# Two heads stored by GpSimd in four row pieces, and mask codes of the upper nodes in eight rows: a tree attention kernel on one Trainium2 core

## The chip, the core and the metric

The kernel runs on one core of a Trainium2 chip. The core has a tensor engine for matrix products (PE in the profile; PEld is its weight load, which overlaps the products), a vector engine (DVE), a scalar engine (ACT), GpSimd (POOL) and a sync engine (SP) that here only issues transfers. The engines work on SBUF, a memory of 128 partitions; products land in PSUM. Inputs and output lie in the chip's main memory, and 16 DMA engines move data between it and SBUF. A DMA is issued by SP, ACT or POOL, which each have a queue of their own, and signals through a semaphore when its data has landed. The metric is the device time of one execution in microseconds (us); less is better.

## What is computed

The reference is attention with a tree mask: 8 batches of 12 heads, 512 positions, dimension 64, all fp32. Positions are the nodes of a binary tree in heap order, and each position sees itself and its ancestors only.

```python
    for i in range(seq):
        mask[i, i] = 1
        parent = i
        while parent > 0:
            parent = (parent - 1) // 2
            mask[i, parent] = 1

    scores = np.einsum('bhqd,bhkd->bhqk', Q, K) * scale
    scores = scores + (1 - mask) * (-1e9)
    weights = np.exp(scores - np.max(scores, axis=-1, keepdims=True))
    weights = weights / (np.sum(weights, axis=-1, keepdims=True) + 1e-10)
    return np.einsum('bhqk,bhkd->bhqd', weights, V).astype(np.float32)
```

## The kernel before

The 96 heads are worked off as 48 pairs. `Q`, `K` and `V` are loaded by GpSimd with a cast to bf16, heads in groups of 2 to 16, into buffers of the pools `loads` and `vloads` (L238 to L302). For each pair the tensor engine transposes the rows of `K` and `Q` (L398 to L549), computes scores in two parts, turns them into outputs with the values (`values`, L650), and the vector engine divides by the sums (`norm`, L692) into the output tiles `ofs`, one per eight heads, fp32.

The mask is made by products, not by an addition. For every node a column of plus and minus 2048 stands for its path from the root, and a row product with the query's path is 0 where the key is an ancestor and far below 0 elsewhere. This product with the codes opens each accumulation in PSUM, and the product of keys and queries is added to it. Keys are split in two parts: the upper nodes (`scores1`: path codes of at most 7 bits and one row more, `k1code` or `k1wide` with `q1code`) and the nodes below (`scores2`: four tiles with ten rows of codes each, 40 in all, `k2code` or `k2wide` with `q2code`). `_mask_codes` (L71) makes one table of 1536 columns; its first `CODE_ROWS` = 40 rows are loaded into the tile `codes` by two DMAs of SP, 32 and 8 rows (L190). ACT then copies the 40 rows to partitions 64 to 103, since the two heads of a pair use partitions 0 and 64 upwards: 1280 columns at the start (L214), the last 256 at the step "W" (L881). For the later pairs, `far_codes` (L390) makes a copy of the query codes in another column order; both halves of the partitions and both parts make four copies on ACT (L822). The upper part's products take all 40 rows (L567 to L572), of which rows 8 to 39 of `k1` and `q1` are zero.

The order of the work is written out by hand: `FIRST` and the string in the main loop (L861 to L867) give the steps of each pair, and `pool_program` (L725) is one list of all that GpSimd does: loads, copies of values (`spread_pool`, `spread_top`), copies of staged rows (`lay_beside`) and stores. `pool(i)` (L843) takes items off the head of this list as long as `ready` (L773) allows it, so GpSimd's order is fixed. A store of GpSimd takes eight heads of all 128 partitions, 1 MB: in the output each partition holds 1 KB of a head. A store waits until `norm` has written its heads.

Heads 72 to 79 are handled apart. Their pairs are (72, 76), (73, 77), (74, 78) and (75, 79). `store_apart` (L719), called after pair step 38, lets SP store heads 72 and 73 early, each in two DMAs of partitions 0 to 115 and 116 to 127. GpSimd stores the other six heads, 74 to 79, in one DMA (L762 to L765: `n` is 2 there). Its last store is that of heads 80 to 87. Heads 88 to 95 are stored by SP (L897 to L903) and, the very last, by ACT (L904), pair by pair.

Of the kernel before, what the change touches and what calls it, by code (L numbers as in the profile page):

```python
# [9 lines left out]

CODE = 2048.0
CODE_ROWS = 40
NOUT = 22
BEHIND = 56

# [55 lines left out]
def _mask_codes():  # L71
# [5 lines left out]
    k1 = np.zeros((64, 128), np.float32)  # L77
    q1 = np.zeros((64, 4, 128), np.float32)
# [20 lines left out]
    for t in range(4):  # L99
# [4 lines left out]
        for p in range(128):  # L104
            node = 4 * p + t
            query(q1, 0, 7, (PLACE[t], p), node)
            if p >= 32:
                query(q2, 10 * (SELF[t] if p < 64 else t), 9, (PLACE[t], p), node)
    return np.concatenate([k1, q1.reshape(64, -1), k2, q2.reshape(64, -1), k1w, k2w], axis=1)


EYE = ((0, 1, 2), (2, 3, 2), (6, -2, -1), (0, 3, 2), (1, 2, 1))
# [7 lines left out]
def kernel(  # L120
# [7 lines left out]
    nc = tc.nc  # L128
# [26 lines left out]

    perm_dram = nc.inline_tensor(_eye_twice().astype(ml_dtypes.bfloat16), name="tree_eye")
    code_dram = nc.inline_tensor(
        _mask_codes()[0:CODE_ROWS].astype(ml_dtypes.bfloat16), name="tree_codes"
    )

    ctx.enter_context(tc.manual_schedule())
# [25 lines left out]
    first_load(nc.sync, "K", Kr)  # L187
    nc.scalar.dma_start(out=ptile[:, :], in_=perm_dram.ap())
    first_load(nc.scalar, "Q", Qr)
    for r0, r1 in ((0, 32), (32, CODE_ROWS)):  # L190
        nc.sync.dma_start(out=codes[r0:r1, :], in_=code_dram.ap()[r0:r1, :])
    eye = ptile[:, 0:256]

    def eye_blocks(first, x, y):
# [5 lines left out]
    qperm, *perms = [eye_blocks(*e) for e in EYE]  # L200
    k1code = codes[:, 0:128]
    q1code = codes[:, 128:640]
    k2code = codes[:, 640:768]
    q2code = codes[:, 768:1280]
    k1wide = codes[:, 1280:1408]
    k2wide = codes[:, 1408:1536]

    idle = consts.tile([P, 512], bf16)
# [2 lines left out]
    nc.vector.memset(warm[:, :], 0.0)  # L211
    nc.scalar.activation(out=warm[:, :], in_=warm[:, :], func=AF.Exp, scale=scale)

    nc.scalar.copy(out=codes[64:64 + CODE_ROWS, 0:1280], in_=codes[0:CODE_ROWS, 0:1280])  # L214

    NV = 2
    NE = 3
# [171 lines left out]

    def far_codes(p0, k):  # L390

        src = codes[p0:p0 + CODE_ROWS, 128:129]
        return nc.scalar.copy(
            out=far[p0:p0 + CODE_ROWS, k, :, :],
            in_=bass.AP(src.tensor, src.offset + 640 * k, [list(src.ap[0]), [1, 4], [4, 128]]),
        )

    def transpose_one(dst, i, a, t, units, st, perm):  # L398
# [164 lines left out]
    def scores1(i):  # L563

        sp = psS.tile([P, 2, 512], fp32, name="s1")
        for a in range(2):
            nc.tensor.matmul(  # L567
                out=sp[:, a, :],
                lhsT=(k1code if i < WIDE else k1wide)[64 * a:64 * a + CODE_ROWS, :],
                rhs=(q1code, q1wide, q1far)[(i >= WIDE) + (i >= FAR)][64 * a:64 * a + CODE_ROWS],  # L570
                start=True, stop=False,
            )  # L572
        for a in range(2):
            nc.tensor.matmul(  # L574
                out=sp[:, a, :], lhsT=keys(i, a, TOP),
                rhs=qTs[i][64 * a:64 * a + 64, :, :].rearrange("p t c -> p (t c)"),
                start=False, stop=True,
            )
        et = etpool.tile([P, 2, 4, 128], bf16, name="e1")
        nc.scalar.activation(  # L580
            out=et[:, :, :, :].rearrange("p a t c -> p (a t c)"),
            in_=sp[:, :, :].rearrange("p a c -> p (a c)"),
            func=AF.Exp, scale=scale,
        ) if i < WIDE else nc.scalar.activation(  # L584
            out=et[:, :, :, :].rearrange("p a t (r u) -> p a (t r) u", u=2 if i < FAR else 4),
            in_=sp[:, :, :].rearrange("p a (u c) -> p a c u", u=2 if i < FAR else 4),
            func=AF.Exp, scale=scale,
        )
        ets[i] = et
# [125 lines left out]


    APART, APART_AT, APART_ROWS = 72, 38, 116

    def store_apart():  # L719

# [4 lines left out]
    def pool_program():  # L725
# [35 lines left out]
                stored += KB  # L761
        ops.insert(-1, (lay_beside, "qst", 80 // KB))  # L762
        while stored < NH - KB:
            n = 2 if stored == APART else 0
            ops.append((store, nc.gpsimd, stored + n, KB - n))  # L765
            if stored == 40:
                ops.append((lay_beside, "kst", 80 // KB))
            if stored == 64:
# [96 lines left out]
    for i in range(NP + 1):  # L865
        steps = FIRST[i] if i < len(FIRST) else "SVK" if i % 2 else "SVQ"
        steps = "SQVK" if i == FAR - 1 else steps  # L867
        for step in steps:
# [9 lines left out]
            if step == "Q" and qdone < NP:  # L878
                qdone = turn("qst", qdone)
            if step == "W":  # L880
                nc.scalar.copy(  # L881
                    out=codes[64:64 + CODE_ROWS, 1280:1536], in_=codes[0:CODE_ROWS, 1280:1536]
                )
            if step == "X":
                spin("s1" if valued else "ob", 2)
            if step == "D":
# [48 lines left out]
```

## Time and profile before

| | |
|---|---|
| time of the runs, us | 133.29, 133.81, 133.81 (median 133.81) |
| the profiled execution's own time, us | 133.37 |
| its span, first to last instruction, us | 131.6 |
| mean granted clock of the tensor engine | 0.975 of full speed |
| packets moved by DMA | 27959, 32.25 MB |
| main memory | 37.94 MB read, 12.58 MB written, 384 GB/s over the span |

The profile is of one execution. Its page gives the busy time of each engine, the span in 40 equal slices with one digit per slice (tenths busy), DMA queues, the chain of work that ended last, the costliest groups of instructions and the DMA issues with their time to landing. Other views group instructions by line, list waits, show a stretch of time in order, or give the busy times of all engines and the DMA engines' mean share for chosen windows. The DMA share in windows adds up the durations of packets; where packets overlap on one engine, it passes 1.

### The profile page before, as it was taken

The page shows a single profiled execution, that of the slowest core. Times are in us where ns is not written, and L with a number is a line of the kernel's source. Part 1 is how long each engine was busy: PE and PEld are TensorE (multiplying, and loading weights), DVE is VectorE, ACT ScalarE, POOL GpSimd, SP SyncE. Part 2 cuts the span into 40 slices and gives each one's busy share as a digit, 9 for nine tenths or more (in the row PEclk, how much of TensorE's full clock was granted, in tenths as well). Part 3 has the DMA queues.
Part 4 walks back from the last instruction along what each step waited for, and adds up shares of the span by engine and source line. Part 5 has one row for each costly group of instructions (what it writes and reads, how often), then busy time and mean ns, then how long its engine had stood idle before and what let it go on. Part 6 is the DMA issues. An engine that isn't in the chain of part 4 may idle for free.

```text
span 131.6 us, 5430 instructions
## 1 busy us (share of the span) xinstructions
PE 114.2 (87%) x2350; PEld 79.7 (61%) x2353; DVE 104.3 (79%) x254; ACT 101.1 (77%) x163; POOL 83.2 (63%) x114
## 2 busy tenths in 40 slices
PE   6985999999899897899999897896999999999800
PEld 2451676667567566677677674675676777666500
DVE  3528769988999998989899889898799977973620
ACT  4358289989799995968998788796799789899700
POOL 6988726245493999995399899944999945002000
PEclk9998599999999999999999999999999999999995
DMA  4999999999999999999999999999999999999992
GB/s 118 230 176 194 196 199 204 197 205 203 201 204 208 207 207 205 208 207 203 207 207 201 306 270 205 285 291 234 339 218 333 240 291 399 399 402 399 389 342 72
DMA packets 27959, 32.25 MB, mean 245 GB/s; under 512 B 1208, under 2 KB 23096, under 8 KB 27936
## 3 DMA queue, kind: packets, MB, share of 16 engines
q0 software_dynamic: 25760, 29.89, 111.4%
q1 hardware_dynamic: 1616, 1.57, 3.5%
q10 hardware_dynamic: 560, 0.46, 1.2%
q8 instruction: 18, 0.29, 0.8%
q14 instruction: 5, 0.04, 0.1%
HBM read 37.94 MB, written 12.58 MB: 384 GB/s over the span
## 4 chain that ended last, share of the span: by engine, by line
PE 34%; DVE 25%; DMA 16%; ACT 8%; POOL 7%; issue 5%; ACTq 0%; POOLq 0%
PE ob L662 12%; DMA kst<-in_K_dram 11%; DVE of L701 8%; DVE vt L371 6%; DMA qst<-in_Q_dram 5%; ACT e L618 4%; PE s L567 4%; POOL vt L371 3%; ACT e L584 3%; PE s L574 3%; DVE rec L699 2%; PE s L601 2%; PE ktp L477 2%; DVE kq L486 2%; PE s L612 2%
## 5 line engine op out<-in xcount | busy, mean ns | idle before, releaser
L584 ACT ACTIVATE e<-s 128x1024 bf16<-128x1024 f32 x40 | 40.9, 1022 | 13.0 <-PE s L574 12.5
L662 PE MATMUL ob<-vt,e 128*128 128x65 bf16 (+1 forms) x940 | 37.6, 198 | 1.6 <-DVE of L701 1.2
L662 PEld LDWEIGHTS <-e 128*128 128x128 bf16 (+1 forms) x960 | 30.5, 103 | 9.9 <-PE s L612 1.3
L371 POOL COPY vt<-vst 32x512 int32<-32x512 int32 (+4 forms) x44 | 32.5, 739 | 4.8 <-PE ob L662 2.6
L618 ACT ACTIVATE e<-s 128x384 bf16<-128x384 f32 x80 | 34.7, 491 | 0.0
L701 DVE TENSOR_TENSOR of<-ob,rec 128x512 f32<-128x512 f32 x47 | 32.5, 692 | 1.6
L371 DVE COPY vt<-vst 32x1024 bf16<-32x1024 bf16 (+5 forms) x47 | 22.0, 467 | 2.4 <-DMA vst<-in_V_dram 1.6
L699 DVE RECIPROCAL rec<-ob 128x8 f32<-128x8 f32 x47 | 9.6, 205 | 11.1 <-PE ob L662 9.7
L574 PE MATMUL s<-qq,kq 64*128 64x512 bf16 x80 | 15.3, 377 | 0.0
L709 POOL DMA_DIRECT2D out_dram<-of x11 | 9.8, 895 | 8.5 <-DVE of L701 8.0
L612 PE MATMUL s<-qq,kq 64*128 64x160 bf16 (+1 forms) x320 | 14.9, 208 | 0.1
L612 PEld LDWEIGHTS <-kq 64*128 64x128 bf16 x320 | 12.4, 94 | 4.2 <-issue 0.3
L601 PEld LDWEIGHTS <-codes 40*128 40x128 bf16 x80 | 6.4, 95 | 10.5 <-issue 4.9
L567 PE MATMUL s<-far,codes 40*128 40x512 bf16 x64 | 12.5, 386 | 0.1
L254 POOL DMA_DIRECT2D qst<-in_Q_dram x12 | 8.5, 704 | 5.6 <-DMA kst<-in_K_dram 2.9
L543 DVE COPY qq<-qtp 128x1024 bf16<-128x1024 bf16 x16 | 10.9, 683 | 1.0 <-PE qtp L538 1.0
L580 ACT ACTIVATE e<-s 128x1024 bf16<-128x1024 f32 x8 | 8.2, 1022 | 4.6 <-PE s L574 4.6
L371 ACT COPY vt<-vst 32x512 int32<-32x512 int32 (+3 forms) x19 | 10.4, 545 | 1.4 <-DMA vst<-in_V_dram 1.0
L601 PE MATMUL s<-far,codes 40*128 40x384 bf16 x64 | 10.6, 324 | 0.6 <-ACT e L618 0.5
L254 POOL DMA_DIRECT2D kst<-in_K_dram x11 | 8.5, 775 | 4.1 <-DMA vst<-in_V_dram 1.8
L477 PE MATMUL ktp<-ptile,kst 128*64 128x128 bf16 x256 | 9.9, 220 | 0.9 <-DMA kst<-in_K_dram 0.6
L538 PE MATMUL qtp<-ptile,qst 128*64 128x128 bf16 x192 | 7.4, 220 | 2.9 <-DMA qst<-in_Q_dram 2.0
(56 smaller groups left out, 155.3 us busy)
## 6 DMA issues: line engine op xcount, KB each, us to landing
out_dram<-of POOLq DMA_DIRECT2D x10, 1024.0 KB, 15.4
kst<-in_K_dram POOLq DMA_DIRECT2D x9, 512.0 KB, 14.3
qst<-in_Q_dram POOLq DMA_DIRECT2D x8, 512.0 KB, 16.2
vst<-in_V_dram POOLq DMA_DIRECT2D x12, 256.0 KB, 13.7
vst<-in_V_dram POOLq DMA_DIRECT2D x6, 512.0 KB, 12.7
qst<-in_Q_dram POOLq DMA_DIRECT2D x6, 256.0 KB, 12.4
kst<-in_K_dram POOLq DMA_DIRECT2D x4, 256.0 KB, 9.7
out_dram<-of POOLq DMA_DIRECT2D x1, 768.0 KB, 14.7
```

Of the source, the lines that this page charges most:

```text
L254: return nc.gpsimd.dma_start(out=kept[b][:, h0 % KB:h0 % KB + n, :, :].rearrange("p (g x) t d -> p g (x t d)", x=x), in_=src[:, h0 // x:(h ...
L371: return copy(out=dst, in_=src)
L477: nc.tensor.transpose(out=columns(kp[64 * a:64 * a + 64, :], mixed, *dims), in_=st[:, place[a], 4 * u + t, :], identity=ptile[:, 0:128],)
L567: nc.tensor.matmul(out=sp[:, a, :], lhsT=(k1code if i < WIDE else k1wide)[64 * a:64 * a + CODE_ROWS, :], rhs=(q1code, q1wide, q1far)[(i >= ...
L574: nc.tensor.matmul(out=sp[:, a, :], lhsT=keys(i, a, TOP), rhs=qTs[i][64 * a:64 * a + 64, :, :].rearrange("p t c -> p (t c)"), start=False, ...
L584: ) if i < WIDE else nc.scalar.activation(
L601: nc.tensor.matmul(out=flat[:, a, :, :].rearrange("p u (t c) -> p u t c", t=4)[:, :, :, 32 // n:], lhsT=k2wide[64 * a:64 * a + CODE_ROWS, ...
L612: nc.tensor.matmul(out=flat[:, a, :, lo:hi], lhsT=keys(i, a, WTILE2[t]), rhs=qT[64 * a:64 * a + 64, :, lo:hi], start=False, stop=t == 1, s ...
L618: nc.scalar.activation(out=e2s[i % NE][:, a, :, 32:128].rearrange("p t (r u) -> p t r u", u=n), in_=flat[:, a, :, :].rearrange("p u (t r) ...
L662: nc.tensor.matmul(out=ob[lo:hi, a, 65 * t:65 * t + 65], lhsT=e[:, a, PLACE[t], lo:hi], rhs=vt[vtile[tile_v][0]][:, head(i, a) % VB, vtile ...
L699: nc.vector.reciprocal(out=rec[:, a:a + n, :, :], in_=o4[:, a:a + n, :, D:D + 1])
L701: nc.vector.tensor_tensor(out=ofs[j][:, h0:h1 + 1:head(i, 1) - head(i, 0), :, :], in0=o4[:, a:a + n, :, 0:D], in1=rec[:, a:a + n, :, :].to ...
```

## The change

Two things are changed.

The six-head store of GpSimd becomes five DMAs: heads 74 to 77 of all partitions in one, and heads 78 and 79 together in four pieces (`PIECES`) of partitions 0 to 4, 5 to 8, 9 to 124 and 125 to 127, that is 5, 4, 116 and 3 rows.

The codes of the upper part are kept as `PATH_ROWS` = 8 rows: they stand in columns 0 to 767 of the tile (`k1`, `q1`, `k1wide`), those of the lower part in columns 768 to 1535 (`k2`, `q2`, `k2wide`). SP loads them in two DMAs, 8 rows and 48 rows of 768 columns (of the 48 rows 40 are used). ACT doubles each part by itself, `double`, with 8 and 40 rows, 640 columns at the start and 128 at the step "W". Two of the four `far_codes` copies and the products of `scores1` take 8 rows instead of 40. A product takes as many columns as before.

```diff
--- before.py
+++ after.py
@@ -10,6 +10,7 @@
 
 CODE = 2048.0
 CODE_ROWS = 40
+PATH_ROWS = 8
 NOUT = 22
 BEHIND = 56
 
@@ -106,7 +107,9 @@
             query(q1, 0, 7, (PLACE[t], p), node)
             if p >= 32:
                 query(q2, 10 * (SELF[t] if p < 64 else t), 9, (PLACE[t], p), node)
-    return np.concatenate([k1, q1.reshape(64, -1), k2, q2.reshape(64, -1), k1w, k2w], axis=1)
+    upper = np.concatenate([k1, q1.reshape(64, -1), k1w], axis=1)
+    lower = np.concatenate([k2, q2.reshape(64, -1), k2w], axis=1)
+    return np.concatenate([upper[0:PATH_ROWS], lower[0:48]], axis=0)
 
 
 EYE = ((0, 1, 2), (2, 3, 2), (6, -2, -1), (0, 3, 2), (1, 2, 1))
@@ -155,7 +158,7 @@
 
     perm_dram = nc.inline_tensor(_eye_twice().astype(ml_dtypes.bfloat16), name="tree_eye")
     code_dram = nc.inline_tensor(
-        _mask_codes()[0:CODE_ROWS].astype(ml_dtypes.bfloat16), name="tree_codes"
+        _mask_codes().astype(ml_dtypes.bfloat16), name="tree_codes"
     )
 
     ctx.enter_context(tc.manual_schedule())
@@ -187,8 +190,8 @@
     first_load(nc.sync, "K", Kr)
     nc.scalar.dma_start(out=ptile[:, :], in_=perm_dram.ap())
     first_load(nc.scalar, "Q", Qr)
-    for r0, r1 in ((0, 32), (32, CODE_ROWS)):
-        nc.sync.dma_start(out=codes[r0:r1, :], in_=code_dram.ap()[r0:r1, :])
+    nc.sync.dma_start(out=codes[0:PATH_ROWS, 0:768], in_=code_dram.ap()[0:PATH_ROWS, :])
+    nc.sync.dma_start(out=codes[0:48, 768:1536], in_=code_dram.ap()[PATH_ROWS:PATH_ROWS + 48, :])
     eye = ptile[:, 0:256]
 
     def eye_blocks(first, x, y):
@@ -200,9 +203,9 @@
     qperm, *perms = [eye_blocks(*e) for e in EYE]
     k1code = codes[:, 0:128]
     q1code = codes[:, 128:640]
-    k2code = codes[:, 640:768]
-    q2code = codes[:, 768:1280]
-    k1wide = codes[:, 1280:1408]
+    k1wide = codes[:, 640:768]
+    k2code = codes[:, 768:896]
+    q2code = codes[:, 896:1408]
     k2wide = codes[:, 1408:1536]
 
     idle = consts.tile([P, 512], bf16)
@@ -211,7 +214,17 @@
     nc.vector.memset(warm[:, :], 0.0)
     nc.scalar.activation(out=warm[:, :], in_=warm[:, :], func=AF.Exp, scale=scale)
 
-    nc.scalar.copy(out=codes[64:64 + CODE_ROWS, 0:1280], in_=codes[0:CODE_ROWS, 0:1280])
+    ROWS_OF = (PATH_ROWS, CODE_ROWS)
+
+    def double(k, c0, c1):
+        n = ROWS_OF[k]
+        return nc.scalar.copy(
+            out=codes[64:64 + n, 768 * k + c0:768 * k + c1],
+            in_=codes[0:n, 768 * k + c0:768 * k + c1],
+        )
+
+    for k in range(2):
+        double(k, 0, 640)
 
     NV = 2
     NE = 3
@@ -389,10 +402,10 @@
 
     def far_codes(p0, k):
 
-        src = codes[p0:p0 + CODE_ROWS, 128:129]
+        src = codes[p0:p0 + ROWS_OF[k], 128:129]
         return nc.scalar.copy(
-            out=far[p0:p0 + CODE_ROWS, k, :, :],
-            in_=bass.AP(src.tensor, src.offset + 640 * k, [list(src.ap[0]), [1, 4], [4, 128]]),
+            out=far[p0:p0 + ROWS_OF[k], k, :, :],
+            in_=bass.AP(src.tensor, src.offset + 768 * k, [list(src.ap[0]), [1, 4], [4, 128]]),
         )
 
     def transpose_one(dst, i, a, t, units, st, perm):
@@ -566,8 +579,8 @@
         for a in range(2):
             nc.tensor.matmul(
                 out=sp[:, a, :],
-                lhsT=(k1code if i < WIDE else k1wide)[64 * a:64 * a + CODE_ROWS, :],
-                rhs=(q1code, q1wide, q1far)[(i >= WIDE) + (i >= FAR)][64 * a:64 * a + CODE_ROWS],
+                lhsT=(k1code if i < WIDE else k1wide)[64 * a:64 * a + PATH_ROWS, :],
+                rhs=(q1code, q1wide, q1far)[(i >= WIDE) + (i >= FAR)][64 * a:64 * a + PATH_ROWS],
                 start=True, stop=False,
             )
         for a in range(2):
@@ -715,6 +728,7 @@
 
 
     APART, APART_AT, APART_ROWS = 72, 38, 116
+    PIECES = ((0, 5), (5, 9), (9, 125), (125, P))
 
     def store_apart():
 
@@ -761,8 +775,12 @@
                 stored += KB
         ops.insert(-1, (lay_beside, "qst", 80 // KB))
         while stored < NH - KB:
-            n = 2 if stored == APART else 0
-            ops.append((store, nc.gpsimd, stored + n, KB - n))
+            if stored == APART:
+                ops.append((store, nc.gpsimd, stored + 2, 4))
+                for p0, p1 in PIECES:
+                    ops.append((store, nc.gpsimd, stored + 6, 2, 1, p0, p1))
+            else:
+                ops.append((store, nc.gpsimd, stored, KB))
             if stored == 40:
                 ops.append((lay_beside, "kst", 80 // KB))
             if stored == 64:
@@ -878,9 +896,8 @@
             if step == "Q" and qdone < NP:
                 qdone = turn("qst", qdone)
             if step == "W":
-                nc.scalar.copy(
-                    out=codes[64:64 + CODE_ROWS, 1280:1536], in_=codes[0:CODE_ROWS, 1280:1536]
-                )
+                for k in range(2):
+                    double(k, 640, 768)
             if step == "X":
                 spin("s1" if valued else "ob", 2)
             if step == "D":
```

## The prediction

> **What bounds the kernel now.** I read the page's slices first, then the DMA queues, then busy times in chosen windows of the tail.
>
> ```profile
> span 131.6 us, 5430 instructions
> PE 114.2 (87%) x2350; PEld 79.7 (61%) x2353; DVE 104.3 (79%) x254; ACT 101.1 (77%) x163; POOL 83.2 (63%) x114
> DMA  4999999999999999999999999999999999999992
> GB/s 118 230 176 194 196 199 204 197 205 203 201 204 208 207 207 205 208 207 203 207 207 201 306 270 205 285 291 234 339 218 333 240 291 399 399 402 399 389 342 72
> ```
>
> No compute engine is full, but the DMA digit is 9 from the second slice to the last but one. The window rows below give length, busy time of PE, PEld, DVE, ACT and POOL, granted clock, share of the 16 DMA engines (packets that overlap count twice, so it can pass 1) and GB/s.
>
> ```profile
> 2.50:10.00 7.50, 6.66 (x68) 3.41 (x67) 2.58 (x6) 3.72 (x5) 7.11 (x10) 1.00 1.30 215
> 10.00:60.00 50.00, 45.23 (x960) 31.78 (x962) 45.03 (x110) 41.48 (x66) 34.24 (x51) 0.97 1.31 203
> 60.00:104.00 44.00, 40.71 (x924) 29.51 (x922) 39.31 (x90) 37.25 (x63) 35.09 (x43) 1.00 1.19 255
> 104.00:118.00 14.00, 13.91 (x286) 10.34 (x284) 11.55 (x29) 11.87 (x20) 4.48 (x5) 1.00 1.07 356
> 118.00:122.00 4.00, 3.85 (x72) 2.42 (x72) 1.87 (x5) 3.83 (x8) 0.89 (x1) 1.00 1.02 402
> 122.00:124.00 2.00, 1.81 (x40) 1.21 (x36) 0.95 (x4) 1.97 (x5) 0.00 (x0) 1.00 1.02 391
> ...
> 124.00:126.00 2.00, 0.76 (x16) 0.52 (x14) 1.78 (x5) 0.20 (x1) 0.00 (x0) 1.00 0.96 368
> 127.50:128.00 0.50, 0.00 (x0) 0.00 (x0) 0.00 (x0) 0.00 (x0) 0.00 (x0) 1.00 0.86 299
> 128.00:128.50 0.50, 0.00 (x0) 0.00 (x0) 0.00 (x0) 0.00 (x0) 0.00 (x0) 0.98 0.72 248
> 128.50:129.00 0.50, 0.00 (x0) 0.00 (x0) 0.00 (x0) 0.00 (x0) 0.00 (x0) 0.50 0.54 189
> 129.50:129.70 0.20, 0.00 (x0) 0.00 (x0) 0.00 (x0) 0.00 (x0) 0.00 (x0) 0.50 0.32 113
> 129.85:130.30 0.45, 0.00 (x0) 0.00 (x0) 0.00 (x0) 0.00 (x0) 0.00 (x0) 0.50 0.07 23
> ```
>
> From 2.5 to 124 us the share is never below 1: the 16 DMA engines work without a break, and compute hides behind them. The last compute ends near 126, yet packets move for 4 us more. There the engines stop one after another: 0.32 x 16 is five engines at 129.6, and 0.07 x 16 is one engine, alone until 130.3. So the end is set by how much the most loaded DMA engine has to carry. A byte taken off that engine, anywhere after 2.5 us, shortens the kernel; compute does not.
>
> No view prints single engines, but the trace keeps each increment of a DMA's semaphore. From those records, in us of the span (the first number of an SP piece is one update at its issue):
>
> ```
> head 72, rows 0-115, SP:    104.75 | 114.28 114.47 114.51 114.61
> head 72, rows 116-127, SP:  107.22 | 111.19 111.22 111.24 111.24 111.35 111.70 111.84 111.84
>                                      120.40 120.56 120.62 120.65
> last DMA, 128 rows, ACT:    127.63 127.64 127.75 128.19 128.48 128.74 128.80 128.95
>                             129.24 129.25 129.38 130.03 130.05 130.11 130.15 130.68
> ```
>
> A 128-row DMA is split over sixteen engines, the 116-row piece over four (116 = 4 x 29), the 12-row piece over twelve. Four of the twelve came 9 us late: they stood behind the 116-row pieces. I call these four 0 to 3, the other eight 4 to 11, and the four without a row 12 to 15. At the end four engines have 2.5 to 3 us to spare, one works 0.5 us longer than any other.
>
> **The change part by part.** Its first part concerns the store of heads 74 to 79 by GpSimd.
>
> ```profile
> 110.74 0.84 POOL L709 DMA_DIRECT2D out_dram<-of  x1 [0.45 <-DVE of L701]
> 119.11 0.89 POOL L709 DMA_DIRECT2D out_dram<-of  x1 [7.53 <-DVE of L701]
> ...
> out_dram<-of POOLq DMA_DIRECT2D x1, 768.0 KB, 14.7
> ```
>
> Before, each engine carries 8 rows of 1 KB for each of heads 78 and 79, 16 KB. If GpSimd splits as SP did, 5, 4, 116 and 3 rows go to 5, 4, 4 and 3 engines, just sixteen: twelve "light" engines carry one row of each head, 2 KB, four "heavy" ones 29 rows, 58 KB. At 402 GB/s an engine moves 25.1 KB/us. A light engine saves 14 x 1024 B = 0.57 us, a heavy one pays 42 x 1024 B = 1.71 us.
>
> Which four are heavy decides, and no row shows GpSimd split a DMA. Dealt out in order from the first engine, the 116 rows fall on 9 to 12: three engines of the eight and one of the four without a row. The early four are of this make-up. Between three successive completions of 1 MB stores (108.44 to 113.85 us in the packet records) the leading three took 2.584 + 2.675, 2.626 + 2.632 and 2.584 + 2.584 us: the first two carried two extra rows of some 46 ns each, the third none. The fourth has a 12-row piece's mark at 111.884, just before its own at 111.890. I take 9 to 12. The early four then end at 127.63 + 1.71 = 129.34 up to 128.19 + 1.71 = 129.90, the last engine at 130.68 - 0.57 = 130.11: it stays last, and the whole 0.57 counts. The bounds are +1.71 (a heavy last engine) and -0.57.
>
> The Trainium skill, "DMA: Bandwidth & Descriptors", section "Why a DMA increments its semaphore by 16 and not by 1", says the same of the split (the largest number up to 16 that divides the rows), and that GpSimd takes consecutive engines from a cursor that moves round; no run here shows the cursor; started at the first engine it gives the sum below. It also reports some GpSimd copies cut into sixteenths instead, which is rival B.
>
> Five issues replace one. Nearest rows are 0.84 and 0.89 us, so four more cost POOL 3.4 to 3.6 us, in the 7.53 us for which it waited for DVE anyway. The program adds three waits, for semaphores used again: the 116-row piece waits for the store issued at 100.15, the 3-row piece for the next, the store of heads 80 to 87 for the first of three issued at 102.92. In order:
>
> ```profile
> 100.15 1.80 POOL L709 DMA_DIRECT2D out_dram<-of  x2
> out_dram<-of POOLq DMA_DIRECT2D x1, 1024.0 KB, 11.6
> out_dram<-of POOLq DMA_DIRECT2D x2, 1024.0 KB, 12.5
> ...
> 102.92 2.64 POOL L709 DMA_DIRECT2D out_dram<-of  x3
> out_dram<-of POOLq DMA_DIRECT2D x1, 1024.0 KB, 14.1
> ```
>
> These landed at 111.8, 114.4 (the median 12.5 makes the second 13.4) and 117.0, so POOL is done with the pieces near 115.3 and free for 119.11. Only that last store is queued behind them. The old store took 14.7 us to land, so the engines have work queued. Cost nothing; without this cover, an engine idle until a late issue, up to 0.9 per issue.
>
> Four more DMAs mean four more completion marks per engine: at least nothing, at most a 1 KB row each (4 x 0.041 = 0.16). A mark is four bytes, so I take 0.03.
>
> The same page, section "Anatomy of one DMA", gives a DMA a fixed cost of about 2.0 us, mostly the wait for the write's receipt. In line, four more would be 8 us, and the sum +7.4; the share of 1.02 while stores are queued speaks against that.
>
> The second part is the codes.
>
> ```profile
> codes<-tree_codes SPq DMA_DIRECT2D x1, 96.0 KB, 3.2
> codes<-tree_codes SPq DMA_DIRECT2D x1, 24.0 KB
> L214 ACT COPY codes<-codes x1: 1257/1257/1257, 5.6 to 5.6; 40x1280 bf16<-40x1280 bf16 x1
> L881 ACT COPY codes<-codes x1: 402/402/402, 25.8 to 25.8; 40x256 bf16<-40x256 bf16 x1
> L393 ACT COPY far<-codes x4: 647/660/664, 36.2 to 46.1; 40x512 bf16<-40x512 bf16 x4
> L567 PE MATMUL s<-far,codes x64: 373/386/387, 51.8 to 121.7; 40*128 40x512 bf16 x64
> L574 PE MATMUL s<-qq,kq 64*128 64x512 bf16 x80 | 15.3, 377 | 0.0
> ```
>
> Loaded are 8 x 1.5 + 48 x 1.5 = 84 KB for 96 + 24 = 120 KB. The 36 KB less are 0.09 us over the engines, and since these stay full afterwards, that reaches the end; bounds 0 (if the gap at the start swallows it) and 0.09. Copies go by columns, not rows: the line through 402 ns at 256 and 1257 at 1280 gives 0.72 us at 640 and 0.30 at 128, so ACT pays 1.44 for 1.26 and 0.59 for 0.40. A product's time does not grow from 40 rows (386 ns) to 64 (377), so 8 rows cost about the same; below that no row exists, and a gain on PE would be hidden. All of it lies under the full DMA engines: nothing; uncovered, 0.4 us.
>
> Sum: -0.57 + 0.03 - 0.09 = -0.63 us. The profiled execution took 133.37 us, 1.8 beyond its span, so 132.74. The runs were 133.29, 133.81 and 133.81: the sum's basis lies 0.44 under their median, which itself would give 133.18. Of the four times the mean is 133.57; I forecast 133.57 - 0.63 = 132.94.
>
> **The rivals.** A, slower: the 116 rows fall on other engines, because the dealing starts elsewhere. It decides as soon as a heavy engine's end above is past 130.68 - 1.71 + 0.06 = 129.03, true for eight of sixteen. On engines 0 to 3: 130.15 + 1.65 = 131.80, so +1.12 and 134.7; on the three near 129.3: +0.35, 133.9; on the last one: +1.65, 135.2. For it: no row shows GpSimd's start. Against: the make-up of the early four.
>
> B, no change: 116 rows are dealt eight to an engine. Then thirteen or more engines carry what they did, the first few up to three rows of both heads more (6 KB, 0.25 us: 130.40 on engines 0 to 3, still under 130.68). Only the codes and the marks count, -0.06: 133.5. The rows 0-115 of SP speak against it, but for SP only.
>
> C, a new wait: the store of heads 80 to 87 is held by its semaphore. It would have to land 2.1 us later than before to matter; then up to 1 us of idle engines, 134.5.
>
> **How the numbers follow.** Forecast 0.68, A 0.18, B 0.10, C 0.04. Faster by over 0.5%, about what a measurement here can tell from no change, means under 133.14. The forecast's own range is 132.4 (the last engine's extra 0.5 gone as well) to 133.3; four fifths lie under 133.14, so faster 0.54. Same: the rest of the forecast 0.14, most of B 0.09, A's mild landing 0.04, so 0.27; slower 0.19. The range runs from 132.3 to 134.2, past B and A's mild case, and leaves out the heavy landings.
>
> **What would show it.** Right: the window rows of the tail lose their single engine near 129.7, the share falls more steeply after 128, the last packet comes 0.6 us earlier, and the 116-row piece shows four late increments from engines that led. Wrong in the placing: a share of 0.25, four engines, stands alone at the end past 130.7. B: the tail rows look as before. C: POOL's last store starts after 119.1 with a DMA as releaser. The codes step is right if the first loads land about 0.1 us sooner and ACT's first copies take 0.7 us each. The forecast fails if the DMA share drops under 1 before 124.

## The result and the profile after

The changed kernel took 134.16 us in the median of 22 runs (133.31 to 143.45), the kernel before 133.17 us in 22 runs beside them. Three of the 22 runs, and 12 of the 36 runs of three other kernels below with products of 8 rows, but none of a kernel without them, were disturbed (over 1.5% longer than the fastest, at granted clocks of 0.81 to 0.96); every ratio leaves these out, while the medians are of all runs. The ratio is 1.0057, 95% interval [1.0042, 1.0073]: some 0.76 us slower, where 0.63 us faster was forecast. The profiled execution took 133.54 us with a span of 131.8 us.

From the page of the changed kernel, with the line of the chain from the page of before at the end:

```profile
span 131.8 us, 5438 instructions
PE 118.5 (90%) x2353; PEld 79.8 (61%) x2353; DVE 105.8 (80%) x254; ACT 101.4 (77%) x165; POOL 86.2 (65%) x118
DMA  3999999999999999999999999999999999999894
GB/s 107 236 175 191 202 194 200 202 201 206 199 205 210 205 206 206 210 208 200 210 205 202 316 258 207 298 276 250 316 226 326 246 298 399 400 406 363 328 336 149
DMA packets 28263, 32.22 MB, mean 244 GB/s; under 512 B 1488, under 2 KB 23432, under 8 KB 28240
PE 58%; DVE 24%; DMA 5%; ACT 4%; POOL 3%; issue 3%; ACTq 0%; POOLq 0%
...
PE 34%; DVE 25%; DMA 16%; ACT 8%; POOL 7%; issue 5%; ACTq 0%; POOLq 0%
```

Three things differ from the page of before. The last slices of GB/s were 402 399 389 342 72 and are now 406 363 328 336 149: the engines move less from the slice that begins at 118.6 us on, and more at the very end. PE is busy for 118.5 instead of 114.2 us. And the chain that ended last is 58% PE and 5% DMA, where it was 34% and 16%. The same windows of the tail (columns as in the prediction):

```profile
118.00:122.00 4.00, 3.86 (x72) 2.54 (x69) 2.79 (x7) 3.52 (x7) 0.47 (x1) 1.00 0.96 366
122.00:124.00 2.00, 2.00 (x43) 1.26 (x41) 0.90 (x2) 1.84 (x4) 0.47 (x1) 1.00 0.86 303
124.00:126.00 2.00, 1.95 (x42) 1.20 (x39) 0.90 (x2) 1.90 (x5) 0.00 (x0) 1.00 1.00 385
...
127.50:128.00 0.50, 0.00 (x0) 0.00 (x0) 0.47 (x3) 0.00 (x0) 0.00 (x0) 1.00 0.71 246
128.00:128.50 0.50, 0.00 (x0) 0.00 (x0) 0.47 (x3) 0.00 (x0) 0.00 (x0) 1.00 0.90 313
128.50:129.00 0.50, 0.00 (x0) 0.00 (x0) 0.10 (x1) 0.00 (x0) 0.00 (x0) 1.00 0.88 307
...
129.50:129.70 0.20, 0.00 (x0) 0.00 (x0) 0.00 (x0) 0.00 (x0) 0.00 (x0) 1.00 0.98 345
129.85:130.30 0.45, 0.00 (x0) 0.00 (x0) 0.00 (x0) 0.00 (x0) 0.00 (x0) 1.00 0.35 116
```

The share of the 16 DMA engines is 0.96 from 118 to 122 us and 0.86 from 122 to 124, where it was 1.02 and 1.02. The prediction had named a share under 1 before 124 as what would make it fail. DVE works until past 128.5 us, where before it ended before 126, so the last stores come later: from 129.5 to 129.7 us and from 129.85 to 130.3 the share is 0.98 and 0.35, where before it was 0.32 and 0.07.

Part of this lateness may belong to the execution that was profiled. Two windows of before, then the same two of the changed kernel; the granted clock is the third value from the end:

```profile
10.00:15.00 5.00, 3.50 (x45) 1.82 (x46) 3.74 (x11) 3.65 (x6) 4.29 (x6) 0.74 1.44 194
15.00:20.00 5.00, 4.99 (x111) 3.75 (x108) 3.98 (x11) 3.19 (x4) 1.75 (x4) 0.92 1.43 198
...
10.00:15.00 5.00, 3.36 (x46) 2.04 (x48) 3.81 (x11) 3.64 (x6) 4.44 (x6) 0.63 1.44 193
15.00:20.00 5.00, 5.00 (x82) 3.10 (x80) 2.88 (x8) 2.03 (x3) 1.38 (x2) 0.68 1.43 199
```

That is 5 x (0.11 + 0.24) = 1.75 us of full clock less than before had: by estimate up to that much of the 2.6 us by which ACT's last store comes later (128.63 us, before 126.03). GpSimd's issues, in its timeline:

```profile
112.85 3.79 POOL L722 DMA_DIRECT2D out_dram<-of  x5 [1.98 <-DVE of L714]
121.53 0.93 POOL L722 DMA_DIRECT2D out_dram<-of  x1 [4.89 <-DVE of L714]
```

The 4-head store and the four pieces take 3.79 us, and the next store still waits 4.89 us for DVE, not for GpSimd's own issues or for an earlier DMA.

### The profile page after: what moved, and what is told of

Same layout as the page of the kernel before. It is cut to its first block, busy times and chain, and to the rows that moved or that the text cites. A ratio compares the mean times of both kernels' runs of the same rounds, so it can differ in the third digit from the quotient of the medians.

```text
span 131.8 us, 5438 instructions
## 1 busy us (share of the span) xinstructions
PE 118.5 (90%) x2353; PEld 79.8 (61%) x2353; DVE 105.8 (80%) x254; ACT 101.4 (77%) x165; POOL 86.2 (65%) x118
## 2 busy tenths in 40 slices
DMA packets 28263, 32.22 MB, mean 244 GB/s; under 512 B 1488, under 2 KB 23432, under 8 KB 28240
## 4 chain that ended last, share of the span: by engine, by line
PE 58%; DVE 24%; DMA 5%; ACT 4%; POOL 3%; issue 3%; ACTq 0%; POOLq 0%
PE ob L675 19%; PE s L587 8%; PE s L580 8%; DVE of L714 7%; DVE vt L384 7%; DMA qst<-in_Q_dram 5%; PE ktp L490 4%; PE s L625 4%; PE s L614 4%; PE qtp L551 3%; DVE rec L712 2%; DVE kq L499 2%; DVE kq L507 2%; DVE kq L503 2%; POOL kst L257 2%
## 5 line engine op out<-in xcount | busy, mean ns | idle before, releaser
L384 DVE COPY vt<-vst 32x1024 bf16<-32x1024 bf16 (+5 forms) x47 | 23.4, 497 | 2.8 <-DMA vst<-in_V_dram 2.0
L722 POOL DMA_DIRECT2D out_dram<-of x15 | 12.9, 860 | 7.0 <-DVE of L714 6.9
L625 PEld LDWEIGHTS <-kq 64*128 64x128 bf16 x320 | 12.1, 94 | 4.2 <-issue 0.2
L580 PE MATMUL s<-far,codes 8*128 8x512 bf16 x64 | 12.4, 384 | 0.1
L587 PEld LDWEIGHTS <-kq 64*128 64x128 bf16 x96 | 4.6, 93 | 11.2 <-issue 10.9
L312 POOL DMA_DIRECT2D vst<-in_V_dram x7 | 5.6, 798 | 5.8 <-DMA vst<-in_V_dram 3.9
```

The costliest lines, as they stand in the source:

```text
L384: return copy(out=dst, in_=src)
L580: nc.tensor.matmul(out=sp[:, a, :], lhsT=(k1code if i < WIDE else k1wide)[64 * a:64 * a + PATH_ROWS, :], rhs=(q1code, q1wide, q1far)[(i >= ...
L587: nc.tensor.matmul(out=sp[:, a, :], lhsT=keys(i, a, TOP), rhs=qTs[i][64 * a:64 * a + 64, :, :].rearrange("p t c -> p (t c)"), start=False, ...
L625: nc.tensor.matmul(out=flat[:, a, :, lo:hi], lhsT=keys(i, a, WTILE2[t]), rhs=qT[64 * a:64 * a + 64, :, lo:hi], start=False, stop=t == 1, s ...
L722: return eng.dma_start(out=Or[p0:p1, h0:h0 + step * (n - 1) + 1:step, :], in_=ofs[h0 // 8][p0:p1, h0 % 8:h0 % 8 + step * (n - 1) + 1:step, ...
```

## The experiments

Each time is a median, each ratio one to the kernel before on the same chip, with its 95% interval.

**The parts alone.** The pieces in the kernel before, its codes untouched:

```
+    PIECES = ((0, 5), (5, 9), (9, 125), (125, P))
-            n = 2 if stored == APART else 0
-            ops.append((store, nc.gpsimd, stored + n, KB - n))
+            if stored == APART:
+                ops.append((store, nc.gpsimd, stored + 2, 4))
+                for p0, p1 in PIECES:
+                    ops.append((store, nc.gpsimd, stored + 6, 2, 1, p0, p1))
+            else:
+                ops.append((store, nc.gpsimd, stored, KB))
```

> The pieces alone, codes as before. Forecast's theory (116 rows on engines that lead): 0.4 to 0.6 us faster than before. Rival A (116 rows on SP's engines 0 to 3, where the completion marks of the profile after seem to put them): those four end near 131.8 in the span, 0.9 to 1.2 us slower than before. Compute: both theories expect the last issue by ACT at 126.0 us of the span, as before.

133.78 us, 1.0039 [1.0017, 1.006]: 0.52 us slower, which neither the forecast's theory (0.4 to 0.6 us faster) nor rival A on engines 0 to 3 (0.9 to 1.2 us slower) had given.

The codes alone (the changed kernel with the old store of six heads):

```
-    PIECES = ((0, 5), (5, 9), (9, 125), (125, P))
-            if stored == APART:
-                ops.append((store, nc.gpsimd, stored + 2, 4))
-                for p0, p1 in PIECES:
-                    ops.append((store, nc.gpsimd, stored + 6, 2, 1, p0, p1))
-            else:
-                ops.append((store, nc.gpsimd, stored, KB))
+            n = 2 if stored == APART else 0
+            ops.append((store, nc.gpsimd, stored + n, KB - n))
```

> The codes alone, the six-head store as before. Theory P (a product of 8 rows makes the following 64-row product start 0.32 instead of 0.23 us after it, 48 times, and the tensor engine falls behind): PE busy 118.5 instead of 114.2, ACT's last issue at 128 to 129 us instead of 126.0, 0.5 to 1.0 us slower than before. Rival K (the lower granted clock of 10 to 20 us in the profile after is chance, and set compute back): PE busy near 114, no change. Forecast: 0.1 us faster.

133.35 us, 1.0004 [0.9977, 1.003]: no difference that this could measure, and the 0.09 us which the prediction gave the smaller load can't be seen in it. PE was busy for 118.0 us, as theory P had it, but the 0.5 to 1.0 us that P gave for this did not come. Most of the slowdown came with the pieces. Windows of the kernel with the pieces alone:

```profile
128.00:129.00 1.00, 0.00 (x0) 0.00 (x0) 0.00 (x0) 0.00 (x0) 0.00 (x0) 0.96 1.03 359
129.00:130.00 1.00, 0.00 (x0) 0.00 (x0) 0.00 (x0) 0.00 (x0) 0.00 (x0) 0.50 0.40 137
130.00:130.50 0.50, 0.00 (x0) 0.00 (x0) 0.00 (x0) 0.00 (x0) 0.00 (x0) 0.50 0.28 96
130.50:131.00 0.50, 0.00 (x0) 0.00 (x0) 0.00 (x0) 0.00 (x0) 0.00 (x0) 0.50 0.04 12
```

All compute has ended, the engines are full until 129 (1.03), and a share of 0.28, between four and five engines, is left after 130, where before it was one, at 0.07 from 129.85 on.

**Splitting, or placing?** By the dealing of the prediction, from the first engine on, four even pieces go over all sixteen engines, and three other splittings put the 116 rows elsewhere. Each is the kernel with the pieces alone and another line:

```
PIECES = ((0, 32), (32, 64), (64, 96), (96, 128))   # four even pieces
PIECES = ((0, 5), (5, 121), (121, 128))             # 116 rows on engines 5 to 8
PIECES = ((0, 12), (12, 128))                       # on 12 to 15
PIECES = ((0, 116), (116, 128))                     # on 0 to 3
```

> The kernel before with heads 78 and 79 stored in four pieces of 32 rows: each goes over all sixteen engines, two rows of each head per engine, so the load is even and no engine is left out. If the slowdown comes from splitting (more DMAs, more completion marks, more issues on GpSimd): 0.3 to 0.5% slower than before, as the pieces 5, 4, 116 and 3. If it comes from uneven loads and tiny packets: within 0.15% of before, and no 16 byte packets in the records.

> The kernel before with pieces of 5, 116 and 7 rows: 116 rows on engines 5 to 8, one row on each other. Placement: two of the four (7 and 8) have 2.5 to 3 us to spare, the other two end as the heavy ones of the pieces 5, 4, 116 and 3 did, near 131.0 us of the span: 0.2 to 0.5% slower than before. Tiny packets alone: the same 0.3 to 0.5%. Splitting alone: three pieces, 0.2 to 0.35%. A time no slower than before would say that engines 5 and 6 have time to spare too.

> The kernel before with pieces of 12 and 116 rows: 116 rows on engines 12 to 15, one row on each other. Placement: one of the four (14 or 15) has time to spare, the others end near 131.0 us or later: 0.2 to 0.8% slower than before, by the marks of those three. Tiny packets alone: 0.3 to 0.5%, as with every place. Splitting alone: two pieces, 0.1 to 0.2%.

> The kernel before with pieces of 116 and 12 rows: 116 rows on engines 0 to 3, which carry SP's 116 rows of head 72 already and end last or next to last before. Placement: they end at 131.3 to 131.8 us, four engines alone at the end for a microsecond: 0.7 to 1.2% slower than before (the prediction's rival gave 134.7 us for this place). Tiny packets alone: 0.3 to 0.5%. Splitting alone: two pieces, 0.1 to 0.2%.

| pieces | engines with 29 rows | time, us | ratio | over before, us |
|---|---|---|---|---|
| 32, 32, 32, 32 | none | 133.47 | 0.9999 [0.9978, 1.002] | 0.0 |
| 5, 4, 116, 3 | 9 to 12 | 133.78 | 1.0039 [1.0017, 1.006] | 0.52 |
| 5, 116, 7 | 5 to 8 | 133.87 | 1.0039 [1.0012, 1.0066] | 0.52 |
| 116, 12 | 0 to 3 | 134.47 | 1.0079 [1.005, 1.0108] | 1.05 |
| 12, 116 | 12 to 15 | 135.04 | 1.0119 [1.008, 1.0159] | 1.59 |

Splitting costs nothing measurable: four even pieces issue as many DMAs and marks as the change. Two pieces in the wrong place cost three times as much as four in a better one, and more than the 0.2 to 0.8% that was expected of them. Placing decides. Windows of the run with the 116 rows on 12 to 15, then of the one on 0 to 3:

```profile
130.00:130.50 0.50, 0.00 (x0) 0.00 (x0) 0.00 (x0) 0.00 (x0) 0.00 (x0) 0.50 0.18 64
130.50:131.00 0.50, 0.00 (x0) 0.00 (x0) 0.00 (x0) 0.00 (x0) 0.00 (x0) 0.50 0.13 45
131.00:131.50 0.50, 0.00 (x0) 0.00 (x0) 0.00 (x0) 0.00 (x0) 0.00 (x0) 0.50 0.10 35
```

```profile
130.00:130.50 0.50, 0.00 (x0) 0.00 (x0) 0.00 (x0) 0.00 (x0) 0.00 (x0) 0.50 0.28 96
130.50:131.00 0.50, 0.00 (x0) 0.00 (x0) 0.00 (x0) 0.00 (x0) 0.00 (x0) 0.50 0.22 76
131.00:131.50 0.50, 0.00 (x0) 0.00 (x0) 0.00 (x0) 0.00 (x0) 0.00 (x0) 0.50 0.10 35
```

Times sixteen, the first has about three engines after 130 us and the second about four. The increments of the semaphore of the DMA that ended last, a store of SP or ACT, say the same more sharply (us of the span, one per engine):

```
before          127.63 127.64 127.75 128.19 128.48 128.74 128.80 128.95
                129.24 129.25 129.38 130.03 130.05 130.11 130.15 130.68
on 9 to 12      129.17 129.18 129.24 129.25 129.25 129.30 129.35 129.47
                129.48 129.72 129.89 130.15 130.83 130.87 130.87 131.13
on 5 to 8       129.54 129.55 129.56 129.58 129.60 129.61 129.62 129.63
                129.64 129.66 129.71 129.92 130.21 130.27 130.29 131.11
on 12 to 15     129.89 129.89 129.90 129.91 129.92 129.93 129.94 129.94
                129.95 129.95 129.97 130.00 130.05 130.64 131.57 132.05
on 0 to 3       129.74 129.78 129.78 129.79 129.80 129.81 129.82 129.83
                129.85 129.91 130.04 130.23 131.04 131.29 131.60 131.84
changed kernel  130.19 130.20 130.21 130.22 130.23 130.24 130.25 130.25
                130.25 130.34 130.35 130.36 130.55 130.66 130.68 130.86
```

With the 116 rows on 9 to 12 four engines stand apart at the end, as many as are loaded; on 0 to 3 again four; on 5 to 8 the count is less clear. On 12 to 15 only three do. The other thirteen marks lie between 129.89 and 130.05 us, so close that these engines must have been waiting for this store, which SP issued at 128.01 us. The fourth loaded engine is hidden among them: less 1.71 us it would have ended by 128.34, which in the row of before only the four early ones did. (SP's last three issues took 0.9, 0.9 and 0.7 us here and 0.3 to 0.4 before; why, these runs do not show.) Take off the 1.71 us that the prediction gave a heavy engine, and 9 to 12 would have ended at 129.1 to 129.4 us, three of 12 to 15 at 128.9, 129.9 and 130.3, 0 to 3 at 129.3 to 130.1: middle and late marks of the row of before. (The executions are not the same, so this holds to a few tenths, and the marks name no engine: which one is meant follows from the count and the dealing.)

In the profiled execution of the changed kernel itself the two causes meet. ACT issued the last store at 128.63 us, twelve engines ended within 0.17 us of each other, as if they had only waited for it, and four more, as many as are loaded, followed within 0.5 us. That execution says little of how much the placing costs by itself; the kernels with the pieces alone do.

**Where the dealing puts the pieces.** Two kernels with one run each, again with another line of pieces:

```
PIECES = ((0, 6), (6, 8), (8, 124), (124, 126), (126, 128))
PIECES = ((0, 5), (5, 7), (7, 9), (9, 125), (125, 128))
```

> Heads 78 and 79 in 6, 2, 116, 2 and 2 rows, codes as before; one look. If GpSimd deals the rows out over consecutive engines from the first (5, 4, 4 and 3 engines in the pieces run): 6 rows on engines 0 to 5, 2 on 6 and 7, 116 on 8 to 11 with 29 rows each, 2 on 12 and 13, 2 on 14 and 15. The packet records then tell which piece the leading engines take part in. If two leaders are 6 and 7 they carry the second piece; if one is 8 it carries the 116 rows. Time: 133.3 to 134.1.

> Heads 78 and 79 in 5, 2, 2, 116 and 3 rows, codes as before; one look. By the same dealing 5 rows on engines 0 to 4, 2 on 5 and 6, 2 on 7 and 8, 116 on 9 to 12, 3 on 13 to 15. Two leaders should carry the second or the third piece and one the last; the 116 rows lie on the same engines as in the pieces run, so the time is 133.8 within 0.4.

133.85 and 134.23 us, 1.0 and 1.4 us over the one run of before beside them (132.82). Following single engines through the packet records (each packet's start against the end of the one before), I read that engines 7 and 8 are the other two which lead. Such chains are a reading of records which name no engine, and no run here settles it.

**The idea with the leaders as read.**

```
PIECES = ((0, 7), (7, 81), (81, 87), (87, 128))     # 37 rows on 7 and 8, 41 on 15
```

> The kernel before with other pieces for heads 78 and 79: 7, 74, 6 and 41 rows, so that by the dealing seen so far (a run of consecutive engines from the first one, as many as the largest number up to 16 that divides the rows) engines 0 to 6 and 9 to 14 carry one row of each head, engines 7 and 8 carry 37 rows each and engine 15 carries 41. Theory (the slowdown of the changed kernel comes from putting 58 KB on four engines that had no time to spare; the engines with 2.5 to 3 us to spare at the end are 7, 8 and 15): the same idea aimed at them gains, because they take (37 - 8) x 2 KB and (41 - 8) x 2 KB more, about 2.4 and 2.7 us at 25.1 KB/us, and still end with or before the field, while thirteen engines lose 14 KB, less some 0.3 us of small packets of the four extra DMAs: 0.1 to 0.4 us faster than before, the last marks lying between 129.7 and 130.5 us of the span. If the leader is 14 and not 15: engine 15 ends near 132.5, one engine alone at the end, and the time is 1.5 to 2 us over before. Rival (the cost is that of splitting a store in four, wherever the rows fall): 0.3 to 0.5% slower than before, as with the pieces 5, 4, 116 and 3.

135.05 us, 1.0124 [1.0093, 1.0155]: a miss. The time is what the expectation gave for a wrong leader, 1.5 to 2 us over, but not the sign of it, one engine alone at the end: the last five marks are 131.80, 132.28, 132.34, 132.40 and 132.41 us. Its packets and windows:

```profile
DMA packets 28631, 32.26 MB, mean 242 GB/s; under 512 B 1872, under 2 KB 23760, under 8 KB 28608
```

```profile
121.00:123.00 2.00, 1.87 (x44) 1.20 (x38) 1.04 (x3) 1.97 (x4) 0.00 (x0) 1.00 1.16 351
123.00:125.00 2.00, 1.91 (x48) 1.40 (x42) 0.90 (x2) 1.41 (x3) 0.00 (x0) 1.00 1.14 197
125.00:127.00 2.00, 0.00 (x0) 0.00 (x0) 1.12 (x4) 0.00 (x0) 0.00 (x0) 0.87 0.75 276
```

From 123 to 125 us the engines count as busy (1.14) and move 197 GB/s, half of the 391 to 402 of before from 118 to 124 us: ordinary 4 KB packets, 0.165 us in the median, took up to 2.5 us. Around that stretch, from 120.5 to 126.3 us, 552 packets of 16 bytes passed. Whether these slow the others was not tried alone, so this run says nothing certain on the leaders.

**Easing the late ones.** If a fixed engine among 12 to 15 ends last, taking rows off it should gain (engine numbers again by the dealing):

```
PIECES = ((0, 120), (120, 128))   # 15 carries 1 row
PIECES = ((0, 98), (98, 128))     # 14 and 15 carry 2
PIECES = ((0, 104), (104, 128))   # 13 to 15 carry 2
PIECES = ((0, 72), (72, 128))     # 12 to 15 carry 4
```

> The kernel before with heads 78 and 79 in pieces of 120 and 8 rows: engine 15 carries 1 row of each head instead of 8 (14 KB less, 0.57 us), engines 0 to 6 carry 9 (0.08 us more), the others 8. If 15 is the one that ends last, at 130.68 us: the next, at 130.15 us, sets the end, 0.35 to 0.5 us faster than before (0.3%). If the last one is another of 12 to 15, or if no fixed engine is last: within 0.1% of before.

> Pieces of 98 and 30 rows: engines 14 and 15 carry 2 rows instead of 8 (0.49 us less), 0 to 12 carry 9, 13 carries 7. If 14 or 15 ends last: 0.3 to 0.45 us faster (0.3%). Otherwise within 0.1% of before.

> Pieces of 104 and 24 rows: engines 13 to 15 carry 2 rows instead of 8 (0.49 us less), 0 to 8 carry 10 (0.16 us more), 9 to 12 carry 8. If 13, 14 or 15 ends last: the engines 0 to 3 then set the end at 130.3 us, 0.2 to 0.4 us faster (0.2%). If 12 is the last, or none is: the same as before or up to 0.16 us slower.

> Pieces of 72 and 56 rows: engines 12 to 15 carry 4 rows instead of 8 (0.33 us less), 0 to 9 carry 10 (0.16 us more), 10 and 11 carry 6. If any of 12 to 15 ends last: 0.2 to 0.35 us faster (0.2%). If no fixed engine is last: the same as before or up to 0.16 us slower.

133.56, 133.20, 133.09 and 133.26 us; 1.0012 [0.9992, 1.0032], 0.9999 [0.9979, 1.0018], 0.9992 [0.9971, 1.0014], 0.9995 [0.9973, 1.0017]. None gains measurably; for the last two the expected 0.2% lies just inside the interval, for the first two the expected 0.3% does not.

**The products.** The code product of the upper nodes over 8 rows in the kernel before:

```
-    lhsT=(...)[64 * a:64 * a + CODE_ROWS, :],  rhs=(...)[64 * a:64 * a + CODE_ROWS],
+    lhsT=(...)[64 * a:64 * a + 8, :],          rhs=(...)[64 * a:64 * a + 8],
```

> Only the products of the upper codes take 8 rows instead of 40 (the 32 dropped rows are zero); loads, copies and stores as before. P: the whole effect of the codes is here: the second product 0.32 us behind the first, PE busy 118.5, ACT's last issue at 128 to 129, as slow as the codes alone within 0.3 us. If the new DMA shapes or the extra ACT copies are the cause: as before, 126.0 and 133.2.

133.42 us, 0.9989 [0.9959, 1.0018]. The changed kernel with 40, 32 and 33 rows, and once more as it is:

```
PATH_ROWS = 40
PATH_ROWS = 32
PATH_ROWS = 33
PATH_ROWS = 8
```

> The change, but with 40 rows for the upper codes in load, copies and products; two DMAs for the codes and the pieces stay. P: the products are 0.23 us apart again, PE busy near 114.2, ACT's last issue at 126.0, and the time is that of the pieces alone within 0.3 us. If layout and the extra copies are the cause: ACT's last issue at 128 or later.

> The changed kernel with the code product of the upper nodes over 32 rows instead of 8 (the further rows are codes too, of other nodes, so its output is not the reference's mask). Theory one (the key product starts later behind the code product because the two are of different row tilings of TensorE, 32 rows against 64): 32 rows behave as 8: the key product starts 0.32 us behind the code product, and PE is busy for some 118 us. Theory two (the later start goes with the number of rows that are idle): a value between, 0.25 to 0.30 us and PE 115 to 117 us. The time is that of the changed kernel within the spread of single runs, 133.3 to 134.7.

> The changed kernel with the code product of the upper nodes over 33 rows instead of 8 (the further row is a code of another node, so its output is not the reference's mask). Theory one (row tilings): 33 rows behave as the 40 of before: the key product starts 0.23 us behind the code product, PE is busy for some 114 us. Theory two (number of rows): much as with 32 rows. Its time, set against the changed kernel run beside it: if the 4 us of PE add to the slowdown, it is 0.1 to 0.3% under the changed kernel; if the whole slowdown is that of the pieces, both are 0.3 to 0.6% over the kernel before and no more than 0.1% apart.

> The changed kernel once more, beside the product over 33 rows, for a comparison on one chip: 0.4 to 0.7% slower than before. If it and the kernel with 33 rows are no more than 0.1% apart, what the 8 rows cost PE does not reach the end; if it is 0.2% or more slower than that one, it does.

(Rows 8 to 39 of that block are zeros, so 32 and 33 rows leave the mask as it is, other than two of the expectations say.) Times: 133.95 us, 1.0038 [1.0019, 1.0058] with 40 rows; 133.72 us in one run with 32; 133.65 us, 1.0032 [1.0011, 1.0053] with 33; 134.45 us, 1.0057 [1.003, 1.0085] with 8. First PE's timeline: a code product followed by its key product, before, after, with 32 and with 33 rows. The first column is the start of a pair.

```profile
76.70 0.39 PE L567 MATMUL s<-far,codes 40*128 40x512 bf16 x2
76.93 0.38 PE L574 MATMUL s<-qq,kq 64*128 64x512 bf16 x2
```

```profile
78.94 0.39 PE L580 MATMUL s<-far,codes 8*128 8x512 bf16 x2
79.26 0.39 PE L587 MATMUL s<-qq,kq 64*128 64x512 bf16 x2
```

```profile
78.35 0.39 PE L580 MATMUL s<-far,codes 32*128 32x512 bf16 x2
78.67 0.39 PE L587 MATMUL s<-qq,kq 64*128 64x512 bf16 x2
```

```profile
76.97 0.39 PE L580 MATMUL s<-far,codes 33*128 33x512 bf16 x2
77.20 0.38 PE L587 MATMUL s<-qq,kq 64*128 64x512 bf16 x2
```

The key product starts 0.23 us behind a code product of 40 or 33 rows and 0.32 us behind one of 32 or 8, and so it is in the median of the 48 pairs. One row more, and 0.09 us are gone: 48 pairs make 4.3 us, the difference of PE's busy time between the changed kernel and the one before. From 32 to 33 rows it falls too, by 3.3 us between two executions, from 117.3 to 114.0:

```profile
PE 117.3 (89%) x2350; PEld 79.3 (60%) x2353; DVE 104.3 (79%) x254; ACT 101.3 (77%) x165; POOL 86.1 (65%) x118
```

```profile
PE 114.0 (86%) x2350; PEld 79.6 (60%) x2353; DVE 104.0 (79%) x254; ACT 101.3 (77%) x165; POOL 86.2 (65%) x118
PE 29%; DMA 27%; DVE 16%; POOL 13%; ACT 5%; issue 4%; ACTq 0%; POOLq 0%
```

The Trainium skill, "TensorEngine Tiling (Array Packing)", section "Key Properties", says that changing the tiling mode, not just the tile, drains TensorE. The Trainium skill, on the same page, section "Available Configurations", lists modes with tiles of 128, 64 and 32 rows. The step between 32 and 33 rows agrees with such a drain, if a product takes the smallest mode that holds its rows: 8 rows then fall into the mode of 32, the key products' 64 into the next. The drain itself no trace shows; what the runs show is the start that comes 0.09 us later.

With 33 rows PE is 29% of the chain that ended last, with 8 it is 58%. How far the 4 us come through to the last store is less clear. ACT issues it at 125.9 us with 33 rows and at 128.6 with 8, but at 127.8 with 40 and at 127.7 with 32. In this order:

```profile
125.93 0.35 ACTq L722 DMA_DIRECT2D out_dram<-of  x1
128.63 0.35 ACTq L722 DMA_DIRECT2D out_dram<-of  x1
127.76 0.35 ACTq L722 DMA_DIRECT2D out_dram<-of  x1
127.68 0.35 ACTq L722 DMA_DIRECT2D out_dram<-of  x1
```

The expectations of 126.0 us with 40 rows and of 128 to 129 us with the codes alone (127.23 came) were both missed. The execution at 128.63 us had a mean granted clock of 0.63 and 0.68 from 10 to 20 us; in the other three the two values make 1.65 or 1.66, as before, instead of 1.31. So two executions with the earlier start of the key product, 33 and 40 rows, are 1.8 us apart, and 40 and 32 rows, which differ in it, 0.1 us.

In the timed runs the changed kernel stands 0.19 and 0.25% over its forms with 40 and 33 rows and 0.18% over the pieces alone, while without the pieces 8 rows cost nothing measurable (1.0004 and 0.9989 above). All these intervals overlap. So the 4 us of PE are shown; that about a quarter of a microsecond of them reaches the end beside the pieces is suggested by the two kernels measured side by side (8 and 33 rows), but not shown.

## Why the prediction was wrong

**What bounds the kernel** was right for the kernel before and for the pieces alone. The end is set by the most loaded DMA engine; four even pieces cost nothing measurable, the same bytes unevenly dealt cost 0.52 to 1.59 us. For the changed kernel it was not the whole: in its profile the share fell under 1 before 124 us, the prediction's own sign of failing.

**The dealing** was right as far as the runs show it: 4 engines for the 116 rows (12 engines were left out of that piece, by the small packets counted in the last section), and pieces that follow one another. That GpSimd's first engine is also SP's first, so that the numbers 0 to 3 mean the same for both, rests on the price of that place alone. The page of the Trainium skill that the prediction named for this, "DMA: Bandwidth & Descriptors", "Why a DMA increments its semaphore by 16 and not by 1", says that GpSimd's cursor moves round; the places above agree, each with its own price, and its other case, the copy cut into sixteenths (rival B), is not seen.

**The step that failed** is "The early four are of this make-up ... I take 9 to 12". Three engines with a row of SP's 12 and one without is what 9 to 12 and the early four have in common, but other sets of four fit as well. The run on 12 to 15 suggests that one of the early ones lies among these, beside three later ones. 9 to 12 were engines of the middle: by their marks, less 1.71 us, they would have ended at 129.1 to 129.4 us and not by 128.19. This is rival A, and its prices fit:

| heavy engines | rival A | measured |
|---|---|---|
| three near 129.3 us | +0.35 | +0.52 (9 to 12) |
| 0 to 3 | +1.12 | +1.05 |
| with the last one | +1.65 | +1.59 (12 to 15) |

All three lie inside the measured intervals (0.23 to 0.80, 0.67 to 1.44 and 1.07 to 2.12 us), so the runs give no reason to doubt the 1.71 us of a heavy engine. Which price belongs to which place was said in advance for 0 to 3 only. The choice of 9 to 12 was not a reading of the trace but a guess of 0.68 on a likeness.

**The light engines' 0.57 us** may not have counted in full even in the right place; no kernel here tried it. In the marks above no light engine of the run on 9 to 12 ends after 130.15 us, where before five ended between 130.03 and 130.68. But before, five engines ended within 0.65 us of each other, and easing up to four engines, 12 to 15, gained nothing measurable: "the whole 0.57 counts" leant on one engine's 0.5 us in one execution. That lone engine returns in other profiles (1.05 us behind the next with four even pieces, 131.22 after 130.17); which one it is, and why, stays open.

**The issues and waits**: 3.4 to 3.6 us more on GpSimd were expected, 2.95 came (3.79 for five against 0.84 for one), and the store behind them waited for DVE, as forecast. Rival C did not come. The 0.03 us for marks left out a second kind of packet (below).

**The codes**: ACT's first copies took 0.72 us each, as worked out from the line through two old copies. They began at 4.18 and 5.10 us, the old one at 5.56, so the codes came sooner by more than the 0.1 us foreseen; in the time of the codes alone neither that nor 0.09 us can be seen.

**The products**: "8 rows cost about the same" holds for the duration of a product (386 ns with 40 rows, 385 with 8) and missed the start of the next. This is the second step that failed: rows that give a product's own duration tell nothing of the change from one shape to the next, here 0.09 us, 48 times. "All of it under the full DMA engines: nothing" held without the pieces (1.0004), with 4 us between the end of compute and the last packet. Beside the pieces the profiled execution, with compute until 128.6 us, has no such cover left; what share of that is the products' stays open, as said above.

## What to carry to other kernels

When the end is set by a spread between DMA engines, an uneven store is worth its bytes only on engines that are known by number: load four neighbouring engines in an experiment and see in its trace how many stand apart at the end, before building on a guess. Even pieces of a store cost nothing measurable here, so splitting and unevenness are to be tried apart. And a matmul that is cut to fewer rows should be read by the start of the next one, not by its own duration. One issue time or one chain from a single execution is no measure of it: here the granted clock between 10 and 20 us differed as well.

## What the runs showed of the hardware

A DMA of GpSimd over fewer than sixteen engines comes with tiny packets, by their count one on each engine left out for each packet of data that one of the others carries. The page of the changed kernel has 1488 packets under 512 B, the one of before 1208. The 280 more are, in the packet records, 64 marks of 4 bytes (four DMAs on sixteen engines), 48 packets of 8 bytes and 168 of 16 bytes. A heavy engine's 58 KB are 14 packets of 4 KB and one of 2 KB, and 12 engines left out times 14 are 168. With 37 and 41 rows per engine (18 and 20 packets of 4 KB), 14 x 18 + 15 x 20 = 552, as counted. Each takes 9 to 11 ns in the records, so an engine also pays for a DMA that it carries nothing of: by estimate 14 or 15 of them, 0.13 to 0.16 us, beside the heavy piece.
